# Attention values with V stationary in a two-layer hybrid decoder trunk

## The chip, the cores and the metric

One NeuronCore of a Trainium2 chip runs the whole kernel. The metric is the device time of one execution, in microseconds (us). TensorE (PE) multiplies and writes to PSUM; its weight loads have a row of their own (PEld). VectorE (DVE), ScalarE (ACT) and GpSimd (POOL) do the elementwise work, and SyncE (SP) issues the loads.

## The reference

A trunk of two layers works on x with 256 tokens and 1024 features, in float32. Cut to what matters:

```python
for l in range(DEPTH):                       # 2
    h = _rms_norm(x, attn_norm[l])
    proj = h @ w_in[l]                       # 1720 columns, split into q, six k/v, gates, latents
    o_a = _nsa(q_a, k_cmp, v_cmp, k_s, v_s, k_w, v_w, gates)   # 8 heads, 2 groups, dim 64
    o_b = _mla(c_q, c_kv, k_r, ...)                            # 8 heads, dim 64 + 32
    mixed = concatenate([_rms_norm(o_a, nsa_out_norm[l]), _rms_norm(o_b, mla_out_norm[l])])
    x = x + mixed @ w_out[l]
    h = _rms_norm(x, mlp_norm[l])
    x = x + square(relu(h @ w_ff1[l])) @ w_ff2[l]              # 4096 wide
return _rms_norm(x, final_norm)
```

NSA mixes three branches by gates: compressed blocks (15 positions), selected blocks and a window; with 256 tokens the last two both cover the causal keys. Every softmax divides by its sum, and gates and group norms act on the attention's output.

## The kernel before

Tokens lie in two tiles of 128 (`t` = 0, 1). Every large product is done in three passes: an operand is split into a high part of reduced precision (float32r) and the rest, a low part, and `mm3` (L350) adds high x high, high x low and low x high. Weights stream through one SP queue in tiles of 128 x 1024 (two chunks of 512 columns), `ask` (L314) cuts each into two pieces; ACT writes the high part (L334), DVE or POOL in turn the low part (L336).

A layer projects h by four blocks of columns (`kcs`, `q`, `kw`, `lat`). It puts q and keys through a rotation and transposes them, compresses keys and values with 16 chunks of small matmuls (`hid`, L949; four tiles of 32 columns of the array beside each other), multiplies the latents up (`ups`), and then does the attention. The output projection and the MLP in four quarters (`up`, `down`) follow.

Attention comes in units of four heads or head branches. `units` (L654) computes scores into PSUM banks of 512 columns; `softmax` (L637) takes maxima on DVE (L640) and exponentials on ACT (L646), which stay unnormalised. The unit then transposes each 128 x 128 block of p on TensorE (`trans`, L379), ACT copies it to SBUF, and `nsa_values` (L698) and `mla_values` (L751) multiply with p^T stationary and V moving:

```python
mm(o[:, a, br, :], pts[a // per][:, ((a % per) * 2 + br) * nk + kt, :], V[:, kt, br, g, :], start=kt == 0, stop=kt == nk - 1)
```

V has 64 features and a column of ones, so a product has 65 columns, tokens in the partitions, and the softmax sum in the 65th column. `nsa_after` (L713) and `mla_after` (L764) take the reciprocal (L719, L768), multiply by the gate and scale the output (`otmp`, `ob`), and POOL adds the branches (`oa`). The compressed branch is one product with 512 columns (L622, `cmp_chain`). `group_chain` (L784) sums squares on ACT, takes the root on POOL, multiplies by it and by a row of gains (`mx`, L800), and transposes the result back for the output projection (`split_into`, L389).

`norm` (L417) multiplies x by gains (L425), which are broadcast over the partitions by a DMA (`gain`, L263), and transposes the result.

The order of TensorE and SP is written by the kernel itself. `Driver` (L168) advances chains by rank with a clock of its own: the main chain has rank 9, norms 0, transposes 1, NSA 3 and 4, compressed branch 3.5, MLA 5 and 6. A chain says how long its result will need on the other engines, and that time is multiplied by 1.8. DVE, ACT and POOL are ordered by the framework's scheduler (L1178).

PSUM has two banks for accumulators, three for scores, two for transposes and one (`pv`) for values.

Of the kernel before, what the change touches and what calls it, by code (L numbers as in the profile page):

```python
# [9 lines left out]
F32 = mybir.dt.float32  # L10
# [6 lines left out]
P = 128  # L17
L = 2
# [25 lines left out]

BLOCKS = {
    "kcs": (512, 512),
    "q": (0, 512),
    "kw": (1024, 280),
    "lat": (1304, 416),
# [56 lines left out]
def _plan():  # L106
    plan = []

    def add(chunks, per, n, split=True):
        plan.extend((min(per, chunks - a), n, split) for a in range(0, chunks, per))  # L110

    for name, (_, n) in BLOCKS.items():
        add(KC, PER_TILE[name], n)
    add(1, 1, 1024)
    add(2, 1, 768)
    add(16, 2, 512, False)
    add(16, 2, 512)
    for q in range(NQ):
        add(32, 2, 512)
    return plan  # L120


PLAN = _plan() * L


def _layer_stream(inp, l):
    out = []
    w_in = inp["w_in"][l]
    for name, (a, n) in BLOCKS.items():
        out += _tiles(w_in[:, a : a + n], PER_TILE[name])  # L130
    for name, parts in (("w_kv_up", (64, 64)), ("w_q_up", (NOPE, ROPE))):

        w = inp[name][l].reshape(-1, H, sum(parts))
        w = np.concatenate([w[:, :, : parts[0]].reshape(-1, H * parts[0]), w[:, :, parts[0] :].reshape(-1, H * parts[1])], 1)
        out += _tiles(w, 1)
    out += _tiles(np.concatenate([inp["cmp_w1_k"][l], inp["cmp_w1_v"][l]], 1), 2)
    for i in range(2):
        for nb in range(2):
            out += _tiles(inp["w_out"][l][i * 512 : i * 512 + 512, nb * 512 : nb * 512 + 512], 2)
# [9 lines left out]
def _pack(inp):  # L149
    arr = {"x": inp["x"].reshape(S, D)}  # L150
    arr["wst"] = np.concatenate([t for l in range(L) for t in _layer_stream(inp, l)])
    names = ("attn_norm", "nsa_out_norm", "mla_out_norm", "mlp_norm", "mla_q_norm", "mla_kv_norm")
    arr["gains"] = np.concatenate([np.concatenate([inp[n][l] for n in names]) for l in range(L)] + [inp["final_norm"]])
# [11 lines left out]
GL = 3 * 1024 + 384  # L165


class Driver:  # L168

    def __init__(self, banks):
        self.t = 0.0
        self.chains = []
        self.done = {}
        self.free = {k: [0.0] * n for k, n in banks.items()}
        self.count = 0

    def spawn(self, rank, gen):
        self.count += 1  # L180
        self.chains.append([rank, self.count, self.t, gen, None])

    def event(self, name, after=0.0):
        self.done[name] = self.t + after * 1.8

    def put(self, bank, after):
        self.free[bank].append(self.t + after * 1.8)

    def ready(self, c):
# [8 lines left out]
    def run(self):  # L198
        while self.chains:
            able = [(self.ready(c), c) for c in self.chains]  # L200
            able = [(r, c) for r, c in able if r is not None]
            first = min(r for r, _ in able)
            self.t = max(self.t, first)
# [4 lines left out]
            c[4] = None  # L208
            try:
                kind, *what = next(c[3])  # L210
            except StopIteration:
                self.chains.remove(c)
                continue
            if kind == "pe":
                self.t += what[0]
                c[2] = self.t + what[1] * 1.8
            elif kind == "rank":
                c[0] = what[0]
            elif kind == "until":
                c[2] = what[0]  # L220
            else:
                c[2] = self.t
                c[4] = (kind, what[0])


@with_exitstack
def trunk(ctx: ExitStack, tc: tile.TileContext, x, wst, gains, pos, cw2, cst, out):
    nc = tc.nc
    mm = nc.tensor.matmul
    E = {"v": nc.vector, "g": nc.gpsimd, "s": nc.scalar}.get  # L230

    def copy(eng, dst, src):
        (nc.scalar.copy if eng == "s" else E(eng).tensor_copy)(dst, src)  # L233

    pool = lambda name, n, **k: ctx.enter_context(tc.tile_pool(name=name, bufs=n, **k))
    const = pool("const", 1)
    raw_p = pool("raw", 6)
    wp = pool("wsplit", 6)
    hl = pool("hl", 13)
    gp = pool("gain", 2)  # L240
    tm = pool("tm", 6)
    at = pool("at", 1)
    pp = pool("pp", 4)
    sm = pool("sm", 4)
    BANKS = {"acc": 2, "s": 3, "tr": 2, "pv": 1}
    psum = {k: pool(f"ps_{k}", n, space=bass.MemoryType.PSUM) for k, n in BANKS.items()}
    dr = Driver(BANKS)

    def urgent():
        return tc.high_priority(offset=100)  # L250
# [4 lines left out]
    X = [const.tile([P, D], F32, name=f"x{t}") for t in range(NT)]  # L255
# [943 lines left out]
```

## Time and profile before

| what | value |
|---|---|
| median of 3 runs | 641.09 us |
| the three runs | 646.26, 639.11, 641.09 us |
| profiled execution, its own time | 646.11 us |
| span of its instructions | 644.3 us |
| mean granted clock of TensorE | 0.986 |
| TensorE busy | 621.4 us (96%) |

The span reaches from the first to the last instruction. "Busy" counts time in which at least one instruction of an engine is under way. Matmuls overlap in the pipeline, so their durations add up to more than that, and the price of one in a row of equals is the distance from start to start. The granted clock is a share of 2.4 GHz; the other level is 1.2 GHz.

### The profile page before, as it was taken

What the parts mean: (1) busy time and instruction counts of PE and PEld (TensorE: products, weight loads), DVE (VectorE), ACT (ScalarE), POOL (GpSimd) and SP (SyncE); (2) the same over time, 40 slices, a digit from 0 to 9 for tenths busy, and PEclk for the clock granted to TensorE, in tenths of its full rate; (3) what the DMA queues carried; (4) which work ended last, traced back from release to release, by engine and by line L of the source; (5) the groups of instructions that cost most, each with busy time, mean ns of one, the idle gap of its engine ahead of it and who ended that gap; (6) DMA issues with size and microseconds to landing.
All of it is one profiled execution on the core that took longest, in us unless ns stands there. A gap on an engine that the chain in (4) does not pass through costs nothing.

```text
span 644.3 us, 10909 instructions
## 1 busy us (share of the span) xinstructions
PE 621.4 (96%) x4099; PEld 548.3 (85%) x4099; DVE 420.4 (65%) x665; ACT 354.6 (55%) x735; POOL 300.4 (47%) x298
## 2 busy tenths in 40 slices
PE   7899899999999999999999889999999999999995
PEld 4697688889889899899888768798998998998985
DVE  4797778675656647558677866866664673764662
ACT  5566667565535546355564475765663654554551
POOL 2675404344553645445466631244544554554351
PEclk8899999999999999999999898999999999999998
DMA  8756733155555655745644665114547565565601
GB/s 306 264 175 206 236 116 100 34 198 173 185 169 191 208 182 166 226 155 186 213 126 134 211 212 199 34 66 149 177 142 220 164 200 174 193 204 176 198 1 66
DMA packets 31732, 108.48 MB, mean 168 GB/s; under 512 B 3776, under 2 KB 4416, under 8 KB 31680
## 3 DMA queue, kind: packets, MB, share of 16 engines
q1 hardware_dynamic: 31392, 107.27, 50.8%
q8 instruction: 32, 0.52, 0.3%
q10 hardware_dynamic: 288, 0.52, 0.2%
q14 instruction: 20, 0.16, 0.1%
HBM read 106.73 MB, written 1.05 MB: 167 GB/s over the span
## 4 chain that ended last, share of the span: by engine, by line
PE 85%; DVE 7%; ACT 4%; DMA 3%; issue 1%; SPq 0%; POOL 0%; POOLq 0%; ACTq 0%
PE acc L352 24%; PE acc L354 24%; PE acc L353 24%; PE tr L384 4%; DVE wlo L336 2%; PE pv L708 2%; DMA raw<-in_wst_dram 2%; PE pv L759 2%; ACT whi L334 1%; PE acc L949 1%; PE s L693 1%; DMA x<-in_x_dram 1%; PE s L746 1%; ACT p L646 1%; DVE qmT L233 1%
## 5 line engine op out<-in xcount | busy, mean ns | idle before, releaser
L336 POOL TENSOR_TENSOR wlo<-raw,whi 128x512 fp32r<-128x512 f32 (+3 forms) x178 | 245.0, 1397 | 221.2 <-ACT whi L334 220.9
L334 ACT CAST whi<-raw 128x512 fp32r<-128x512 f32 (+2 forms) x360 | 201.4, 610 | 113.6 <-PE acc L354 74.7
L336 DVE TENSOR_TENSOR wlo<-raw,whi 128x512 fp32r<-128x512 f32 (+3 forms) x182 | 170.5, 973 | 58.4 <-ACT whi L334 58.3
L352 PE MATMUL acc<-h,whi 128*128 128x256 f32 x512 | 145.3, 284 | 0.0
L354 PE MATMUL acc<-h,wlo 128*128 128x256 f32 x512 | 145.0, 283 | 0.0
L353 PE MATMUL acc<-h,whi 128*128 128x256 f32 x512 | 145.0, 283 | 0.0
L352 PE MATMUL acc<-whi,u 128*128 128x512 f32 (+1 forms) x264 | 101.5, 384 | 0.0
L353 PE MATMUL acc<-wlo,u 128*128 128x512 f32 (+1 forms) x264 | 101.2, 383 | 0.0
L354 PE MATMUL acc<-whi,u 128*128 128x512 f32 (+1 forms) x264 | 101.1, 383 | 0.0
L352 PEld LDWEIGHTS acc<-h,whi 128*128 128x128 f32 x512 | 98.3, 192 | 0.2
L353 PEld LDWEIGHTS acc<-h,whi 128*128 128x128 f32 x512 | 98.3, 192 | 0.2
L354 PEld LDWEIGHTS acc<-h,wlo 128*128 128x128 f32 x512 | 98.3, 192 | 0.0
L1057 DVE TENSOR_TENSOR sq<-relu 128x512 f32<-128x512 f32 x32 | 37.2, 1161 | 38.9 <-ACT relu L1053 38.9
L354 PEld LDWEIGHTS acc<-whi,u 128*128 128x128 f32 x264 | 49.6, 188 | 9.8
L353 PEld LDWEIGHTS acc<-wlo,u 128*128 128x128 f32 x264 | 49.7, 188 | 9.4
L352 PEld LDWEIGHTS acc<-whi,u 128*128 128x128 f32 x264 | 49.7, 188 | 9.3
L1029 DVE SCALAR_TENSOR_TENSOR x<-acc,r,x 128x512 f32<-128x512 f32 (+1 forms) x33 | 24.1, 731 | 49.0 <-PE acc L354 49.0
L1053 ACT ACTIVATE relu<-acc 128x512 f32<-128x512 f32 x32 | 19.0, 594 | 59.3 <-PE acc L354 59.3
L352 PE MATMUL acc<-whi,h 128*128 128x512 f32 (+2 forms) x112 | 41.2, 368 | 0.0
L353 PE MATMUL acc<-wlo,h 128*128 128x512 f32 (+2 forms) x112 | 40.2, 359 | 0.2 <-POOL wlo L336 0.2
L354 PE MATMUL acc<-whi,h 128*128 128x512 f32 (+2 forms) x112 | 39.9, 357 | 0.0
L646 ACT ACTIVATE p<-s,nm 128x128 f32<-128x128 f32 (+1 forms) x96 | 33.9, 430 | 7.9 <-DVE nm L640 4.0
(185 smaller groups left out, 913.3 us busy)
## 6 DMA issues: line engine op xcount, KB each, us to landing
raw<-in_wst_dram SPq DMA_DIRECT2D x178, 512.0 KB, 4.2
raw<-in_wst_dram SPq DMA_DIRECT2D x8, 416.0 KB, 3.3
raw<-in_wst_dram SPq DMA_DIRECT2D x4, 420.0 KB, 3.3
raw<-in_wst_dram SPq DMA_DIRECT2D x4, 384.0 KB, 3.1
x<-in_x_dram SPq DMA_DIRECT2D x4, 256.0 KB, 6.3
g_mix<-in_gains_dram SPq DMA_DIRECT2D x2, 512.0 KB, 5.8
g_mlp<-in_gains_dram SPq DMA_DIRECT2D x2, 512.0 KB, 5.1
g_attn<-in_gains_dram SPq DMA_DIRECT2D x2, 512.0 KB, 3.9
```

The lines of the kernel that those rows point to most:

```text
L334: nc.scalar.copy(hi[:, v], r[:, v])
L336: E(eng).tensor_sub(lo[:, v], r[:, v], hi[:, v].bitcast(F32))
L352: mm(acc, ah, wh, start=start, stop=False, **k)
L353: mm(acc, ah, wl, start=False, stop=False, **k)
L354: mm(acc, al, wh, start=False, stop=stop, **k)
L384: nc.tensor.transpose(tr[:rows, c, :], col, ident)
L646: nc.scalar.activation(p[:, k], s[:, k], AF.Exp, bias=nm[:, a : a + 1], scale=scale)
L708: mm(o[:, a, br, :], pts[a // per][:, ((a % per) * 2 + br) * nk + kt, :], V[:, kt, br, g, :], start=kt == 0, stop=kt == nk - 1)
L759: mm(o[:, r, :], pts[r // per][:, (r % per) * nk + kt, :], VM[:, kt, hb * 4 + r, :], start=kt == 0, stop=kt == nk - 1)
L1029: nc.vector.scalar_tensor_tensor(X[t][:, c], acc, scale, X[t][:, c], op0=OP.mult, op1=OP.add)
L1053: nc.scalar.activation(r, acc, AF.Relu)
L1057: nc.vector.tensor_mul(sq, r, r)
```

## The change

**Values.** V becomes the stationary operand and p^T the moving one. Output is feature-major: features in the partitions, tokens in the columns. V fills 64 columns of the array, so the heads of even and odd place go to the two halves (`tile_position`). Selected and window branch, both key tiles and the compressed branch add into one PSUM tile, as gates and 1/sum are multiplied into p before its transpose; the sum comes from the exponential's own accumulator. A unit now has eight head branches (NSA: one group) or four heads (MLA), two units for each `t` and kind.

**Group scale later.** The output is feature-major already and needs no transposes. Gains act per partition at the eviction; the squares are added over features by a matmul against ones, and 1/rms, a number per token, multiplies the output projection's accumulator (`into_x`).

**Gains.** All gains lie in one small table with features in the partitions. The attention gain is multiplied in after the transposes of x, the MLP gain into the rows of the up weights as they are split (ACT scales the high part; a DVE operation makes the low part). Broadcast loads go, but for the last norm.

**Order.** `Driver` now models each operation of DVE, ACT and POOL by a formula (`_cost`), places it in a gap of that engine's time line, and issues all engines' instructions in the order of this plan; some operations choose DVE or POOL by which ends earlier. The order of the projections stays; the up weights are read behind `hid`; the main chain has rank 9 throughout, the compressed branch rank 2. Buffers: 5 raw tiles where there were 6, 8 for temporaries where there were 6, 14 for layer tensors where there were 13.

The diff, cut to its core:

```diff
+RANK = ((3, 4), (5, 6))
...
+MARGIN = 250.0
...
+    if lane == "v":
+        if op == "reciprocal":
+            return 100 + 6.6 * n
+        if op == "scalar_tensor_tensor":
+            return 140 + 1.25 * n
+        if op == "tensor_scalar":
+            return 110 + 0.9 * n
+        return 80 + 1.25 * n
+    if lane == "s":
+        return 125 + 0.77 * n + (190 if kw.get("accum_out") is not None else 0)
...
-    def event(self, name, after=0.0):
-        self.done[name] = self.t + after * 1.8
...
+    def event(self, name):
+
+        self.done[name] = max(self.t, self.last) + MARGIN
...
-                nc.scalar.activation(p[:, k], s[:, k], AF.Exp, bias=nm[:, a : a + 1], scale=scale)
-            dr.put("s", 2300)
+                scalar.activation(p[:, k], s[:, k], AF.Exp, bias=nm[:, a : a + 1], scale=scale, accum_out=den[:, a : a + 1])
+            dr.put("s")
+            vector.reciprocal(den, den)
+            if gate is not None:
+                dg = den.rearrange("p (r b) -> p r b", b=2)
+                vector.tensor_mul(dg, dg, gate)
+            pa = p.rearrange("p (a k) -> p a k", k=width)
+            either.tensor_mul(pa, pa, den[:, :, None].to_broadcast([P, n, width]))
             return p
...
+                for br in range(2):
+                    for kt in range(nk):
+                        for par in range(2):
+                            rows = slice(par * DK, (par + 1) * DK)
...
+                            mm(o[rows], values_of(kt, br, g), p, start=br + kt == 0, stop=False, tile_position=(0, par * DK), skip_group_check=True)
                 for a in range(2):
...
+                    c = g * 2 + a
+                    mm(o[:, a, :], bd["v"][:, 2 * c : 2 * c + 2, :].rearrange("p h d -> p (h d)"), pctT[t], start=False, stop=True, skip_group_check=True)
...
+            scalar.activation(sq, pv, AF.Square)
+            vector.tensor_mul(o, pv.rearrange("p (c n) -> p c n", c=2), gain(l, "mix", 4 * i + 2 * g, 2))
+            scalar.copy(hi, o)
+            either.tensor_sub(lo, o, hi.bitcast(F32))
+            dr.put("pv")
...
+            mm(ss[:, :1], sqs, ones, start=True, stop=True)
...
+                            mm(o[rows, a, :], VM[:, kt, hb * 4 + h, :], pts[0][:, h * nk + kt, :], start=a + kt == 0, stop=kt == nk - 1, tile_position=(0, par * DK), skip_group_check=True)
...
+                    if g is not None:
+                        scalar.activation(hi[:, v], r[:, v], AF.Copy, scale=g)
...
+                    vector.scalar_tensor_tensor(lo[:, v], r[:, v], g, hi[:, v].bitcast(F32), op0=OP.mult, op1=OP.subtract)
...
-    with tc.manual_schedule(engines={mybir.EngineType.PE, mybir.EngineType.SP}):
+    with tc.manual_schedule():
         dr.run()
```

## Rows read from the trace of the kernel before

**Rows 1.** The page, first part: busy us (share of span) x instructions.
```profile
PE 621.4 (96%) x4099; PEld 548.3 (85%) x4099; DVE 420.4 (65%) x665; ACT 354.6 (55%) x735; POOL 300.4 (47%) x298
```
**Rows 2.** Stages in us from the span's start; the first row names the columns.
```profile
core 0: us, PE busy (x) PEld busy (x) DVE busy (x) ACT busy (x) POOL busy (x), PEclk, DMA share, GB/s
0.00:28.00 28.00, 21.72 (x78) 13.91 (x79) 15.26 (x24) 14.61 (x29) 13.34 (x22) 0.88 0.82 298
52.00:150.00 98.00, 93.77 (x728) 80.31 (x727) 71.58 (x157) 62.59 (x153) 38.32 (x46) 1.00 0.45 149
150.00:345.00 195.00, 195.00 (x1211) 175.95 (x1210) 120.81 (x146) 102.56 (x188) 98.11 (x77) 1.00 0.57 182
362.00:400.00 38.00, 34.39 (x314) 27.74 (x315) 25.25 (x60) 22.57 (x61) 10.68 (x15) 0.91 0.64 215
```
**Rows 3.** Waits of TensorE, whole span: us in total, times, longest us.
```profile
PE pv L708 <- DVE otmp L722: 3.6, 2, 1.8
PE s L354 <- DVE h L394: 2.7, 1, 2.7
PE tr L384 <- DVE h L425: 2.6, 2, 1.7
PE tr L384 <- DVE kT L496: 2.3, 1, 2.3
PE pv L622 <- ACT pt L233: 1.7, 2, 0.9
PE tr L384 <- DVE qT L530: 1.3, 1, 1.3
```
**Rows 4.** Groups by line and form, TensorE: count, busy us, mean ns.
```profile
L708 PE MATMUL pv<-V,pt 128*128 128x65 f32 x192 | 24.0, 275 | 3.6 <-DVE otmp L722 3.6
...
L759 PE MATMUL pv<-VM,pt 128*128 128x65 f32 x96 | 11.6, 271 | 0.0
...
L384 PE MATMUL tr<-idt,mx 128*128 128x128 f32 x32 | 4.8, 273 | 0.0
```
**Rows 5.** The chain that ended last: start us, us it holds, what, how many.
```profile
61.32 0.79 PE acc L949 x24
...
78.58 0.44 PE tr L384 x4
79.02 0.36 PE acc L949 x8
...
83.86 1.73 PE pv L708 x16
...
106.61 0.89 PE s L746 x8
...
112.57 0.86 PE s L746 x4
```
**Rows 6.** Groups by line and form, the other engines: busy us, mean ns, idle before.
```profile
L336 DVE TENSOR_TENSOR wlo<-raw,whi 128x512 fp32r<-128x512 f32 x162 | 153.4, 983 | 54.8 <-ACT whi L334 54.7
...
L394 DVE TENSOR_TENSOR h<-tr,h 128x512 fp32r<-128x512 f32 x16 | 11.0, 685 | 5.9 <-ACT h L393 5.9
...
L791 POOL TENSOR_TENSOR oa<-oa,ocg 128x512 f32<-128x512 f32 x4 | 5.1, 1267 | 0.2
...
L376 ACT ACTIVATION_READ_ACCUMULATOR junk<-x 128x1 f32 x21 | 3.9, 188 | 0.0
...
L719 DVE RECIPROCAL wv<-pv 128x4 f32<-128x4 f32 x16 | 2.8, 177 | 8.5 <-PE pv L708 8.4
```
**Rows 7.** Timeline of DVE at the start: start us, us, operation, idle before.
```profile
5.95 0.69 DVE L425 TENSOR_TENSOR h<-x,g_attn 128x512 f32<-128x512 f32 x1 [5.03 <-DMA g_attn<-in_gains_dram]
```

More of the change, by code (lines that the diff above doesn't have):

```diff
@@ L1 @@
+import heapq
+from bisect import bisect
+from collections import deque
 from contextlib import ExitStack
@@ L48 @@
     "kw": (1024, 280),
-    "lat": (1304, 416),
 }
@@ new lines, in start_of, with work @@
+    def start_of(self, key, cost, at):
+        return self.clock[key].find(at, cost)[1]
+    def work(self, key, op, f, out, ins, kw):
+        read = [a for a in (*ins, *kw.values()) if hasattr(a, "tensor")]
+        name = out.tensor.name
+        cost = _cost(key, op, max(_size(a) for a in (out, *read)), kw)
+        at = max([self.t] + [self.ready.get(a.tensor.name, 0.0) for a in (read if name not in self.slots else [*read, out])])
+        at = self.clock[key].place(at, cost)
+        end = at + cost + 90
+        outs = [out] + ([kw["accum_out"]] if kw.get("accum_out") is not None else [])
+        for a in outs:
+            self.ready[a.tensor.name] = max(end, self.ready.get(a.tensor.name, 0.0))
+        for a in (*outs, *read):
+            self.used[a.tensor.name] = max(end, self.used.get(a.tensor.name, 0.0))
+        self.last = max(self.last, end)
+        self.count += 1
+        heapq.heappush(self.held, (at, self.count, lambda: f(out, *ins, **kw)))
@@ new lines, in flush, with pe @@
+    def flush(self, t=float("inf")):
+        while self.held and self.held[0][0] <= t:
+            heapq.heappop(self.held)[2]()
+    def pe(self, cost, out, read):
+        at = max([self.t] + [self.ready.get(a.tensor.name, 0.0) for a in read if a.tensor.name not in self.shared])
+        if at > self.t:
+            self.stalls.append((self.t, at - self.t, "pe", out.tensor.name, read[-1].tensor.name))
+        self.flush(at)
+        self.t = at + cost
+        self.ready[out.tensor.name] = self.t + 180
+        for a in read:
+            self.used[a.tensor.name] = max(self.t + 60, self.used.get(a.tensor.name, 0.0))
@@ new lines, in trunk, with __getattr__, call @@
+    E = {"v": vector, "g": gpsimd, "s": scalar}.get
+    class Either:
+        def __getattr__(self, op):
+            def call(out, *ins, **kw):
+                read = [a for a in (*ins, *kw.values()) if hasattr(a, "tensor")]
+                n = max(_size(a) for a in (out, *read))
+                at = max([dr.t] + [dr.ready.get(a.tensor.name, 0.0) for a in read])
+                end = lambda e: dr.start_of(e, _cost(e, op, n, kw), at) + _cost(e, op, n, kw)
+                return getattr(E("g" if end("g") <= end("v") + BIAS[0] else "v"), op)(out, *ins, **kw)
+            return call
@@ L727, in nsa_lane, with gate @@
[L727 to L737 removed]
+            def gate(b):
+                par, a0 = b
+                h = g * R + a0 * per * 2 + par
+                return gates[t][:, h : h + 2 * per - 1 : 2, 1:3]
```

1202 lines of the change are left out of this document (663 added, 539 removed).

## The prediction

> **What bounds the kernel now.** I read the page's first part, then the table by stage, then what TensorE waits for, and only then single lines. The page [rows 1] shows TensorE busy for 621.4 of 644.3 us, with DVE, ACT and POOL at 65, 55 and 47%. A busy TensorE can hide waits, so the stages come next [rows 2]. From 150 to 345 us, the MLP of layer 0, TensorE is busy for 195.00 of 195.00 us at full clock while no other engine is above 62%: nothing that happens on DVE, ACT or POOL there can shorten the kernel, and only less TensorE work could. Time is lost in three places. In the start (0 to 28 us) TensorE is idle for 6.3 us, and the granted clock of 0.88 costs 0.12 x 28 = 3.4 us more. In the attention stretch of layer 0 (52 to 150) it is idle for 98 - 93.8 = 4.2 us. In that of layer 1 (362 to 400) it is idle for 38 - 34.4 = 3.6 us, and the clock of 0.91, one stretch at the lower level of 1.2 GHz behind waits, costs 0.09 x 38 = 3.4 us. The waits [rows 3] name the causes: values matmuls behind the eviction of the units before them (`otmp`, 3.6 us), key transposes behind DVE (2.3 and 1.3), the compressed values behind an ACT copy (1.7), and two in the start (2.7 and 2.6). With some 1.3 us of the key wait that lie before 362, the middle has about 12 us to give, the start at most 9.7.
>
> So the bound is TensorE's instruction stream, and the question is what the change takes out of it, and whether the other engines' new order opens more waits than it closes.
>
> **Values with V stationary.** Duration of a matmul in the trace includes its pipeline, so I price by distance in the chain [rows 5]. The old product has 65 moving columns, far too few: 16 records take 1.73 us, 0.108 each, as much as a record of 128 moving columns (8 in 0.89 us, 0.111 each). A float32 matmul leaves two records. Removed [rows 4]: 192 records of L708 and 96 of L759 at 0.108, that is 20.8 and 10.4 us; and 32 transposes of the normalised group at 0.44/4 = 0.11, 3.5 us. Together 34.7 us.
>
> Added, NSA: a layer has 2 groups x 2 branches x 2 head parities = 8 matmuls for t = 0 and 16 for t = 1, each of 256 moving columns, so 96 records in both layers. Alone, such a record takes 0.86/4 = 0.215 [rows 5], 20.6 us in all; but V fills only 64 columns of the array, and the two parities take its two halves. Added, MLA: likewise 96 records, of 128 columns, 10.7 us alone at 0.111. Whether halves run side by side is the disputed price. The nearest row is the compression matmul at L949, four tiles of 32 columns of the array: 24 records take 0.79 us and 8 take 0.36, so 8 more cost 0.215, or 0.027 each, a quarter of the 0.111 that one alone would take. Four tiles run at once; I take two to do so as well: 10.3 + 5.3 us, with 20.6 + 10.7 as the other end and no reason for less than half.
>
> The same rows give the price of entering and leaving that mode: 0.36 - 0.215 = 0.145 us a visit. The change makes 16 visits (4 units for each t and layer): 2.3 us; 0 and 2 x 2.3 are the bounds. The Trainium skill, "TensorEngine Tiling (Array Packing)", Tiling Modes, says that a change of tiling mode drains TensorE; the trace agrees, and a sum without that rule would be 2.3 us better.
>
> The sum of squares over features is now a matmul against ones: 8 in all, 16 records at 0.111, 1.8 us. The compressed branch goes from one product with 512 columns to four with 128, the same columns, nothing. Transposes of x stay, only without a multiplication before them. Added in sum 10.3 + 5.3 + 2.3 + 1.8 = 19.7; **TensorE's stream gets 34.7 - 19.7 = 15.0 us shorter**. It is bound by itself, so this shows in the time, unless new waits eat it.
>
> **The start.** The first multiplication by a gain waits 5.03 us for a broadcast row of gains [rows 7]; now x is transposed as it lands, and the gain comes from a small table at the eviction. 0.5 MB of broadcast leaves the first loads too, 1.7 us at the 298 GB/s of that stage [rows 2]. But 1 MB of x and 2 MB of the first projection's weights must still land, 10 us at that rate, and the first pair waits for the second half of the rows. Bounds: a loss of 3 us (if the constants, which the mask copy on DVE awaits, come later) and a gain of 8; I take 4.
>
> **The other engines.** Each of 36 score banks gets more: the exponentials' sums (96 reads at 0.188 us on ACT, 18 us), a reciprocal (0.177), for NSA a gate product, and one 128x512 product p x 1/sum on DVE or POOL [rows 6]. In return the work after the values goes: `otmp`, `ob`, `ocg`, `mx` and the low part, 8 x 256 + 4 x 256 + 2 x 512 + 4 x 512 + 4 x 512 = 16 x 512 columns a layer on DVE, and `oa` on POOL. ACT's squares and high parts stay what they are in columns. By layer ACT gets 48 x 0.188 = 9.0 us. DVE gets, if POOL takes nothing, 18 products at 0.685 (the rate of L394), 30 reciprocals and gates at 0.177, and 8 evictions with two passes of 256 columns and sums of 0.5: 12.3 + 5.3 + 9.5 = 27, less 16 x 0.685 + 20 x 0.177 = 14.5; so 12.5 us. Set against the 62.6 us of ACT and 71.6 of DVE in the 98 us of layer 0 [rows 2], with some 87 us left for the stretch (98 less half of the 15 and some waits), ACT stands at 82%, DVE at 97%, and POOL, at 38 us, is free for what is moved. So no engine becomes the bound if the plan shifts work to POOL, but the slack is thin.
>
> The price of a DVE product is itself in dispute. Reading PSUM, DVE takes 0.685 for 128x512 (L394); with both inputs in SBUF it takes 0.983 on average (L336) [rows 6]. The Trainium skill, "SBUF — State Buffer", Who interferes with whom, says that a DVE instruction with two SBUF inputs and a GpSimd instruction that reads SBUF shut each other out. The rows agree so far as L336 is dearer by 0.3 us; by that rule the 36 products would cost 35.4 us of DVE and not 24.7. On POOL such a product takes 1.267 (L791).
>
> In the MLP the gain moves into the split of the weights: all low parts of up tiles go to DVE and nearly all others to POOL. DVE had 120.8 us of 195, ACT 102.6, POOL 98.1 [rows 2], so work is shifted between engines at 50 to 62%, up to six tiles ahead. Cover is ample, so 0; if the cover were gone, a late low part would cost its 0.98 us.
>
> **The order.** Before, the wait times given to the TensorE order were stretched by 1.8 and the other engines' order came from elsewhere; now one plan gives all, with 250 ns of margin. A good plan removes most of the 12 us in the middle; a tight one adds waits where DVE is late. Bounds: 12 us gained to 12 lost; I take 6 gained, half, since the causes named in [rows 3] (long DVE queues ahead of a transpose) are what such a plan sees, while DVE's dearer products are what it doesn't: it prices them at 80 + 1.25 x 512 = 720 ns.
>
> **The sum.** 15.0 + 4 + 6 = 25 us. The profiled execution took 646.1 us (span 644.3, 1.8 around it), the slowest of those shown; the median is 641.1. From 646.1 it gives 621.1, from the median 616.1. I predict **616 us**.
>
> **Rivals.**
> *The plan closes nearly all waits.* Start 8 and middle 12 gained: 15 + 20 = 35, 606 us. For it: the waits have few causes, and out projection and up projections are there as filler. Against: loads in the start. Chance 0.25.
> *The order gives nothing.* Only TensorE's work falls, and waits grow by up to 5 us: 626 to 631 us. For it: ACT and DVE get fuller. Chance 0.20.
> *The halves don't run side by side.* 10.3 + 5.3 us more: 632 us. Against it: L949. Chance 0.08.
> *The normalised p is late* (slower). The product stands between exponential and transposes. A bank then comes later by reads, reciprocal, gate and product, 2 x 0.188 + 2 x 0.177 + 0.983 = 1.7 us, on a DVE that is full. If TensorE has nothing ready in 15 of the 36 banks, that is 26 us, which eats the 25; with 20 banks it is 34, and 616 + 34 = 650 us. Against it: units of four kinds lie side by side, and main work fills. Chance 0.08.
> My forecast has 0.39, its own range 610 to 622.
>
> A measurement of this kernel tells about 1% from no change (its three runs spread by 1.1%). Faster by over 1% (under 634.7): all of the first four cases but the edges, 0.84; within 1%: 0.08; slower: 0.08. The range for 8 in 10 reaches down past the good plan and up past the halves: 602 to 638.
>
> **What would show it.** Right: values records of 256 columns at about half of 0.215 us' distance, TensorE's busy time near 600 us, no rows for transposes of `mx`, the MLP still without idle time, TensorE's waits in the middle of 6 us or less. Wrong: values at 0.215; transposes of `p` waiting for DVE or POOL by more than 10 us in total; TensorE idle in the MLP behind low parts; a longer stretch at 1.2 GHz in either attention stage; a first projection that starts later than 10 us.

## The result, and the profile after

The changed kernel takes 671.09 us (median of 3 runs, 669.05 to 672.6) where the kernel before takes 641.09: ratio 1.0448, interval 1.0342 to 1.0554. It is 30 us slower; 25 us faster was forecast.

The first rows of the page of the kernel after answer to [rows 1]; the last one shows the chain that ended last, by engine (in the same row before: PE 85%, DVE 7%, ACT 4%):

```profile
span 669.3 us, 10994 instructions
PE 627.4 (94%) x4011; PEld 541.5 (81%) x4011; DVE 443.3 (66%) x674; ACT 364.3 (54%) x818; POOL 344.2 (51%) x329
...
PE 77%; POOL 7%; DVE 6%; ACT 3%; issue 3%; DMA 3%; SPq 0%; POOLq 0%; ACTq 0%; DVEq 0%
```

TensorE is busy for 6 us more, but that is no sign of more work. Take the span apart. Idle time is the span less the busy time: 644.3 - 621.4 = 22.9 us before [rows 1], 669.3 - 627.4 = 41.9 after. Time lost to the clock is the span times what the mean granted clock is short of 1: 0.014 x 644.3 = 9.0 before (clock 0.986), 0.040 x 669.3 = 26.8 after (0.960). What is left is work at the full 2.4 GHz: 612.4 before, 600.6 after. So TensorE did get 11.8 us less to do, and lost 19.0 us by idling and 17.8 by the clock. Where the clock is low while TensorE idles, this way counts the time twice. Taken over its busy time alone, the clock costs 6.6 us before and 22.9 after in the two traces, and the work falls by 10.3 us. So read 10 to 12 us of work saved.

Where, the table by stage of the kernel after shows (it answers to [rows 2]; a row begins with the stretch in us). The stretches are, for each layer, from the last compression product to the first output product ("the middle"), from there to the first product of the MLP ("the end"), and the MLP of layer 0:

```profile
core 0: us, PE busy (x) PEld busy (x) DVE busy (x) ACT busy (x) POOL busy (x), PEclk, DMA share, GB/s
78.00:116.00 38.00, 27.23 (x153) 22.57 (x154) 30.64 (x68) 22.63 (x64) 19.86 (x18) 0.80 0.35 115
116.00:158.00 42.00, 42.00 (x249) 31.91 (x250) 28.16 (x53) 21.91 (x59) 17.17 (x21) 0.94 0.28 89
158.00:345.00 187.00, 186.90 (x1191) 169.63 (x1190) 121.19 (x138) 100.27 (x174) 87.32 (x66) 1.00 0.56 183
400.00:442.00 42.00, 32.63 (x165) 27.26 (x164) 30.00 (x71) 23.97 (x70) 22.90 (x21) 0.72 0.34 113
442.00:482.00 40.00, 39.37 (x248) 30.65 (x248) 28.13 (x53) 21.66 (x58) 17.37 (x21) 1.00 0.35 106
```

The same two middles and ends in the kernel before, in the same view:

```profile
80.60:115.00 34.40, 33.23 (x258) 29.62 (x251) 26.89 (x75) 22.70 (x57) 10.76 (x12) 1.00 0.28 101
115.00:143.50 28.50, 28.50 (x159) 24.28 (x157) 18.86 (x32) 16.42 (x37) 11.45 (x15) 1.00 0.39 129
394.30:428.60 34.30, 33.13 (x257) 29.52 (x250) 26.80 (x75) 22.59 (x56) 10.75 (x12) 1.00 0.29 98
428.60:457.50 28.90, 28.83 (x160) 24.39 (x158) 19.97 (x32) 16.59 (x37) 11.39 (x15) 1.00 0.39 126
```

The MLP is as full as before. Before, the middle had 1.2 us of idle time in each layer and the full clock. After, it has 10.8 and 9.4 us of idle time, and its clock costs 0.20 x 38 = 7.6 and 0.28 x 42 = 11.8 us (some of it in the idle time). The middle holds 153 matmul records in place of 258 in layer 0; what left it was in part removed and in part comes later, in the end, which grew from 28.5 to 42 us. Attention of both layers is where the time went: the first product of the MLP starts 14 us later than before in layer 0 (157.7 against 143.5 us) and 24 us later in layer 1 (481.9 against 457.5).

The waits of TensorE in the middle of layer 0 (in total, times, longest), after:

```profile
PE tr L643 <- ACT pt L305: 4.2, 1, 4.2
PE tr L643 <- POOL p L305: 1.9, 1, 1.9
PE acc L440 <- DVE rb L305: 1.3, 1, 1.3
PE pv L440 <- DVE kcmp L305: 1.2, 1, 1.2
```

No one cause dominates: a transpose of p stands behind a late copy to SBUF, another behind the normalising product, the latents' queries and the compressed values behind DVE. The chain of the same stretch (start, us it holds, what) shows what they have in common:

```profile
83.18 1.35 DVE wlo L305
84.53 0.96 DVE sg L305
85.51 0.96 DVE sg L305
...
87.24 2.14 DVE wlo L305 x2
89.38 0.10 DVE kcmp L305
89.48 1.34 DVE wlo L305
90.82 0.33 DVE ra L305
91.15 0.34 DVE rb L305
```

From 83.2 to 91.5 the path that sets the end runs on DVE: the rows shown are 7.5 us of it, and 4.8 of these are low parts of weights that stand in DVE's queue between the small steps of the compression and of the rotation. Added up over the whole stretch, the rows of this view put the chain on DVE for 17.1 of 38 us; in the same view of the kernel before, from 80 to 115 us, they put it there for 5.6 of 35, and on TensorE for 17.5 (11.5 of 38 after). So before the change, too, TensorE held only half of the path through this stretch, although it was busy nearly all the time.

### The profile page after: what moved, and what is told of

Its sections match the earlier page's. It is cut to its first block, busy times and chain, and to the rows that moved or that the text cites. A ratio compares the mean times of both kernels' runs of the same rounds, so it can differ in the third digit from the quotient of the medians.

```text
span 669.3 us, 10994 instructions
## 1 busy us (share of the span) xinstructions
PE 627.4 (94%) x4011; PEld 541.5 (81%) x4011; DVE 443.3 (66%) x674; ACT 364.3 (54%) x818; POOL 344.2 (51%) x329
## 4 chain that ended last, share of the span: by engine, by line
PE 77%; POOL 7%; DVE 6%; ACT 3%; issue 3%; DMA 3%; SPq 0%; POOLq 0%; ACTq 0%; DVEq 0%
PE acc L440 66%; PE pv L440 5%; PE tr L643 3%; POOL wlo L305 3%; PE s L440 3%; DMA raw<-in_wst_dram 2%; POOL FT L305 2%; DVE wlo L305 2%; ACT whi L305 1%; DMA x<-in_x_dram 1%; ACT p L305 1%; POOL ra L305 1%; DVE sq L305 1%; POOL h L305 0%; DVE sg L305 0%
## 5 line engine op out<-in xcount | busy, mean ns | idle before, releaser
L440 PE MATMUL acc<-h,whi 128*128 128x256 f32 x1024 | 185.0, 283 | 0.0
L440 PEld LDWEIGHTS acc<-h,whi 128*128 128x128 f32 x1024 | 160.1, 192 | 0.7
L440 PE MATMUL acc<-whi,u 128*128 128x512 f32 (+1 forms) x528 | 160.6, 383 | 0.0
L305 DVE TENSOR_TENSOR wlo<-raw,whi 128x512 fp32r<-128x512 f32 (+4 forms) x87 | 112.4, 1306 | 18.8 <-ACT whi L305 17.4
L305 ACT CAST whi<-raw 128x512 fp32r<-128x512 f32 (+4 forms) x211 | 112.8, 601 | 5.0 <-DMA raw<-in_wst_dram 3.4
L305 ACT ACTIVATE whi<-raw,gcols 128x512 fp32r<-128x512 f32 x128 | 85.2, 715 | 51.4 <-PE acc L440 47.4
L305 DVE SCALAR_TENSOR_TENSOR wlo<-raw,gcols,whi 128x512 fp32r<-128x512 f32 x128 | 103.2, 860 | 10.0 <-ACT whi L305 10.0
L305 POOL TENSOR_TENSOR p<-p,dn 128x512 f32<-128x512 f32 x35 | 38.6, 1106 | 47.5 <-DVE dn L305 42.7
L440 PE MATMUL acc<-whi,m 128*128 128x512 f32 x128 | 47.4, 419 | 0.0
L440 PEld LDWEIGHTS acc<-whi,h 128*128 128x128 f32 x224 | 41.5, 193 | 3.9
```

The source lines that it names most:

```text
L305: heapq.heappush(self.held, (at, self.count, lambda: f(out, *ins, **kw)))
L440: nc.tensor.matmul(out, lhsT, rhs, **k)
```

## The experiments

Each run is timed against the kernel before on the same chip; the ratio to it is given, with its interval, and the kernel after stands at 1.0448 (1.0342 to 1.0554). A difference in us is a difference of ratios times 641, unless said otherwise.

One caution holds for most of the runs. TensorE's order is written by the driver or by the plan, from costs, ranks and due times, so an edit of any of these writes a new order as well. In the traces only e2, e11 (but for its filling), e19 and e20 keep TensorE's order of the kernel after, and only e4 that of the kernel before.

**First guesses: one edit, one culprit.** The change also moved the up weights behind the compression weights in the stream, gave the order of all engines to the plan, and let POOL take the products. One run each:

```diff
@@ e1 @@
+STREAM = ("kcs", "q", "kw", "lat", "ups", "hid")
...
-    for name in ORDER:
+    for name in STREAM:
...
+                up_weights.extend([list(weights(1)), list(weights(2))])
                 yield from hidden()
@@ e2 @@
-    with tc.manual_schedule():
+    with tc.manual_schedule(engines={mybir.EngineType.PE, mybir.EngineType.SP}):
@@ e3 @@
-BIAS = (1000.0, 1500.0, 0.0)
+BIAS = (-1000.0, 1500.0, 0.0)
@@ e4, in the kernel before: plan of the stream, then its use @@
+    add(16, 2, 512, False)
     add(1, 1, 1024)
     add(2, 1, 768)
-    add(16, 2, 512, False)
...
-        wkv = list(weights(1))
-        wq = list(weights(2))
...
+        wkv = list(weights(1))
+        wq = list(weights(2))
         for t in range(NT):
             yield need("latT", t)
```

> The changed kernel with one edit: the three tiles of the latent up projections stand ahead of the compression weights in the stream and are split ahead of the compression matmuls, as in the kernel before. Theory 1 (between the end of the compression matmuls and the output projection TensorE starves for these weights, 20 us idle in both layers, and falls to 1.2 GHz behind that, 20 us more): idle time in that stage drops to 8 us or less in both layers together, the clock's loss to 6 or less, 671 -> about 645 us (637 to 652). Theory 2 (the plan's order of DVE, ACT and POOL is at fault everywhere): at most 6 us better, 665 or more. Theory 3 (products sent to POOL are at fault): no better than 665.

> The changed kernel with one edit: only TensorE and SyncE keep the order of the plan; DVE, ACT and POOL are ordered by the framework's scheduler, as before. Theory 2: most of the loss goes, 650 us or less. Theory 1: the weights still come late, 660 or more. Theory 3: the choice of POOL stays, 665 or more.

> The changed kernel with one number changed: an operation that may go to DVE or POOL goes to POOL only where the plan has it end 1 us earlier there (before: unless it ends 1 us later). Theory 3: the waits of TensorE for kd, qr and p on POOL (10.6 us in all) go and the clock's loss with them, 655 us or less. Theory 1 and 2: within 5 us of 671, as DVE gets what POOL loses.

> The kernel before with the reverse of the first edit alone: the up projections' tiles stand behind the compression weights in the stream. Theory 1: the same stage, 1.2 us idle a layer before, starves by 4 to 8 us a layer, and 641 -> 650 to 660 us. Theory 2 and 3: within 3 us of 641, as the order of the engines and the use of POOL stay.

Measured: e1 672.78 us, 1.0437 (1.0372 to 1.0503); e2 700.09, 1.0870 (1.0800 to 1.0940); e3 681.16, 1.0563 (1.0499 to 1.0627); e4 638.9, 0.9936 (0.9894 to 0.9977). None of the three theories got its gain. The place of the up weights does nothing after the change, and in the kernel before the later place is even a little better: 638.9 us, 0.6% under the kernel before (0.2 to 1.1%), the fastest of this study. With TensorE's order of the plan kept, the plan's order of the other engines is 27 us better than the framework's. Products on DVE, with the new order that this brings, are no better than on POOL (e3; the intervals touch).

**Waiting for the compressed branch.** After the change the compressed branch adds into the same accumulator as the other two, so the NSA values wait for it; the first stand at 105 us (the timeline's first row of `pv<-pt,kv`). e5 takes the wait away, e6 moves the compression up, e7 keeps the computation whole but adds the compressed branch later, and e9 is e6 and e7 together:

```diff
@@ e5 @@
-            if i == 0:
-                yield need("pct", t)
...
-                    mm(o[:, a, :], bd["v"][...], pctT[t], start=False, ...)
+                    mm(o[:, a, :], idt, idt, start=False, ...)
@@ e6 @@
-ORDER = ("kcs", "q", "kw", "lat", "hid", "ups")
+ORDER = ("kcs", "q", "hid", "kw", "lat", "ups")
@@ e7, behind the values of the other branches @@
+                scalar.copy(part, pv)
+                dr.put("pv")
+                yield need("pct", t)
+                yield "get", "pv"
...
+                    mm(pv[:, a * P : a * P + P], bd["v"][...], pctT[t], start=True, stop=True, ...)
+                vector.tensor_add(part, pv, part)
...
```

> The NSA values multiply constants in place of the compressed values and probabilities, same instructions, and no longer wait for them (the output lacks the compressed branch). Theory W (after the change the compressed branch adds into the same PSUM accumulator as the other two branches, so the first NSA values stand at 105 us where they stood at 65, and TensorE lacks work from 76 to 100 and from 400 to 430): first values near 70 us, TensorE's idle 18 to 26 us in place of 35, clock loss 10 to 18 in place of 27, time 640 to 656 us. Rival R (the longer chain from scores to transposes, with its accumulate reads, reciprocals, gates and POOL products, sets the pace): first values earlier, but time within 6 us of 671.

> Only the order of the weight blocks: the compression weights directly behind q, ahead of kw and lat. Theory W: the hidden layer ends some 10 us earlier against the NSA scores, and kw and lat cover its chain; time 650 to 664 us. Rival R: within 6 us of 671.

> The whole computation, but the compressed product has an accumulator of its own and is added on VectorE when it comes; values of the other two branches wait for nothing but their probabilities. Costs 8 copies of 256 columns on ScalarE and 8 additions on VectorE more. Theory W: first values near 70 us, time 642 to 658 us, a few us over the run without the wait. Rival R: 668 to 678 us.

> The compression weights directly behind q and the compressed product added later. Theory W: the wait is gone already with the second, so the order adds little: 640 to 658 us. Rival R: 665 to 678 us.

Measured: e5 668.58 us, 1.0358 (1.0301 to 1.0416); e6 674.78, 1.0462 (1.0404 to 1.0519); e7 665.37, 1.0304 (1.0237 to 1.0372); e9 673.06, 1.0432 (1.0373 to 1.0491). In e7 the values start at 69 us, and the time falls by 0.0144 x 641 = 9 us of 30. In e5 it falls by 6. Both intervals still touch that of the kernel after, and both runs have a new order. The middles of e7:

```profile
77.20:116.60 39.40, 30.87 (x194) 25.72 (x186) 31.43 (x72) 25.07 (x76) 20.64 (x19) 0.83 0.35 120
400.90:440.80 39.90, 31.53 (x197) 26.09 (x185) 30.75 (x74) 25.54 (x75) 21.39 (x20) 0.84 0.33 113
```

The values moved, but the stage takes 39.4 and 39.9 us where it took 38 and 42, with 8.5 and 8.4 us of idle time. So the wait was real, and it isn't what sets the length of the middle.

**Margin, clock, softmax, cover.** Four runs about what that is:

```diff
@@ e10 @@
-MARGIN = 250.0
+MARGIN = 1000.0
@@ e11, where the plan sees TensorE pause in attention @@
+            if self.fill:
+                self.fill(int((at - self.t - 150.0) / 60.0))
...
+            nc.tensor.matmul(pvs[:, 3 * P :], zero, zero, start=True, stop=True, ...)
@@ e12 @@
-            vector.reciprocal(den, den)
...
-            either.tensor_mul(pa, pa, den[:, :, None].to_broadcast([P, n, width]))
@@ e14, in the kernel before, for NSA and MLA values @@
-                        for kt in range(nk):
+                        kt = 0
...
-                return 4 * nk * 107
+                return 4 * 107
```

> One number: the plan lets a result be used 1000 ns, not 250 ns, after its own forecast of its end. Theory M (the plan is too tight: vector work ends later than it thinks, so TensorE stands before instructions that were put too early while later ones could run): TensorE's idle under 28 us in place of 35, time 650 to 664 us. Rival L (TensorE lacks work in the middle of attention whatever the order, because the chains there are longer than the work that is left beside them): 668 to 684 us.

> In attention, from the compression layer on, every pause that the plan forecasts for TensorE is filled with matmuls of zeros by zeros (some 200 a layer, 128 columns each, about 12 us a layer at 2.4 GHz), into columns that nobody reads. Theory C (the idle time costs twice: the clock falls to its lower level in and behind it, and the work that follows takes twice as long; clock loss is 27 us after the change and 9 before): the clock stays at its higher level in the middle, clock loss under 15 us, time 648 to 662 us although TensorE does more. Rival L (the chains between the engines set the end, TensorE's speed there doesn't): 668 to 676 us with the clock up. If the filling comes where there is no pause: 678 to 690 us.

> Left out: the reciprocals of the sums, the gate products and the product of the probabilities with them (36 products of 512 columns, nearly all on POOL at 1.05 us, that stand between exp and the transposes); the output lacks the division and the gates. Theory N (the longer chain from scores to transposes is what holds TensorE): time 648 to 660 us, idle under 27 us. Rival L2 (other chains, from hidden layer to compressed values and from latents to keys and queries, hold it): 664 to 671 us.

> The kernel before, with the value products of the second key tile left out (a third of them: 96 of 288 records, 6.9 us at the mean of 72 ns of the rows); softmax, transposes and everything else stay, and the output lacks those keys. Theory L (the value products were the cover of chains that are as long as the work beside them, so that taking them away gives little): 1 to 3 us less than before. Rival P (before is bound by TensorE's work, and the loss after the change comes from the new order alone): 5 to 8 us less than before.

Measured: e10 679.18 us, 1.0553 (1.0489 to 1.0617); e11 675.01, 1.0491 (1.0436 to 1.0545); e12 659.03, 1.0241 (1.0183 to 1.0299); e14 642.39, 0.9983 (0.9941 to 1.0025).

A wider margin doesn't help. The filling of e11 raised the mean clock from 0.960 to 0.982; its middles, and the end of layer 1:

```profile
78.00:121.00 43.00, 37.36 (x363) 33.28 (x355) 30.89 (x68) 22.51 (x64) 20.08 (x18) 0.88 0.30 102
405.00:446.00 41.00, 34.94 (x361) 30.26 (x358) 30.56 (x71) 23.81 (x70) 23.04 (x21) 1.00 0.33 114
446.00:486.00 40.00, 39.32 (x250) 30.67 (x251) 26.77 (x53) 21.49 (x58) 17.48 (x21) 1.00 0.31 106
```

In layer 1 TensorE runs the middle at full clock, with more than twice the records, and the stage takes 41 us where it took 42; in layer 0 the clock is 0.88 where it was 0.80, and the stage takes 43 us where it took 38. So theory C's 648 to 662 us didn't come: with a higher clock the time is no better. That the clock by itself costs nothing isn't shown, since the filling takes time too, some 25 us at full clock, of which idle time took 8 (41.9 before the filling, 33.8 with it). In one stretch the clock did cost: the records that the kernel after takes from 415.7 to 431.4 us, mostly at half the clock, took 12.5 us in e11 and not 15.7.

e14 asks the same of the kernel before. It takes away 96 records, which at the prediction's 0.108 are 10.4 us (the 72 ns a record of its expectation is too low: in the trace they start 0.110 apart). This gave back 0.0017 x 641 = 1 us (4 at most by the interval). Before, TensorE had hardly any idle time in the middle, and yet it wasn't alone on the path, as its 17.5 us of the chain's 35 say as well. That the chains over the other engines were as long as its work is argued from these two and not shown: each unit of e14 reports a shorter time to the driver, so that TensorE's order changed too, and a worse order can hide a gain. e12 says what made the chains longer: without the normalising, 0.0207 of the time, 13 us, comes back. TensorE's idle time fell only from 41.9 to 37.1 us in it; theory N had expected a fall of 8 or more.

**The same from the other side.** Theory S is now that the longer softmax lengthened chains that were already as long as TensorE's work. e15 takes the sums away too. e16 gives the kernel before the new softmax, without the gates, and leaves TensorE's work as it was. e18 and e8 test a second part: the change lets the latent projection come behind the NSA scores (rank 9, before 2.5).

```diff
@@ e15, beside the edit of e12 @@
-... AF.Exp, bias=nm[:, a : a + 1], scale=scale, accum_out=den[:, a : a + 1])
+... AF.Exp, bias=nm[:, a : a + 1], scale=scale)
@@ e16, in the kernel before @@
+            ... AF.Exp, ..., accum_out=den[:, a : a + 1])
+            nc.vector.reciprocal(den, den)
...
+            nc.gpsimd.tensor_mul(pa, pa, den[:, :, None].to_broadcast([P, n, width]))
...
-                    when.append(dr.t + 1610 * 1.8)
+                    when.append(dr.t + 2710 * 1.8)
@@ e18, in the kernel before @@
-        yield "rank", 2.5
@@ e8, beside the edit of e7 @@
+                if name == "lat":
+                    yield "rank", 2.5
...
```

> As e12_no_normalise, and the exps don't sum: the 96 reads of accumulators (some 220 ns each on ScalarE, 21 us in both layers) go too; the output lacks the sums, the division and the gates. Theory S (the softmax chain as a whole is what the change lost on): 644 to 653 us. Rival T (what remains above before comes from the later latents, the feature-major steps behind the values and the plan's order): 655 to 661 us.

> The kernel before, with the softmax of the kernel after: exps that sum, reciprocals, and a product of 512 columns on POOL for every score bank ahead of its transposes; transposes are allowed 2 us later, the computation is whole, and TensorE's work is that of before. Theory S (softmax chain, whatever the order): 652 to 668 us. Rival T: 641 to 649 us, since before's order has other work to put there.

> The kernel before, with the latent projection at the rank of the other projections, behind the NSA scores, as the change has it. Theory T (later latents make the middle of attention longer): 646 to 658 us. Rival S: within 3 us of before.

> The kernel after, with the latent projection back at the rank of before, ahead of the NSA scores, and the compressed product added later as in e7_compressed_added_later (665 us). Theory T: 648 to 660 us. Rival S: 662 to 672 us.

Measured: e15 673.22 us, 1.0479 (1.0381 to 1.0577); e16 662.87, 1.0331 (1.0252 to 1.0411); e18 658.67, 1.0276 (1.0198 to 1.0354); e8 665.03, 1.0377 (1.0295 to 1.0458).

In e16 nothing is taken from TensorE, the whole computation stays, and the kernel before loses 0.0331 x 641 = 21 us. But the transposes' later due time moves some 380 of TensorE's 4099 records to another place, from 62 us on, so the 21 us are the softmax and a new order together. First its middles, by stage, then the added product and the added reads (count, busy us and mean ns of one):

```profile
76.40:125.20 48.80, 41.80 (x294) 35.79 (x287) 38.04 (x97) 29.83 (x97) 25.44 (x29) 0.93 0.23 84
399.00:446.40 47.40, 41.82 (x296) 36.03 (x288) 35.00 (x93) 29.23 (x94) 23.00 (x27) 0.92 0.19 67
```

```profile
L651 POOL TENSOR_TENSOR p<-p,dn 128x512 f32<-128x512 f32 x36 | 37.3, 1044 | 31.5 <-DVE dn L649 27.1 <-DVE otmp L726 2.0 <-DVE wc L624 1.7
L647 ACT ACTIVATION_READ_ACCUMULATOR p<-s,nm 128x1 f32 x96 | 20.3, 211 | 0.0
```

The middle grows from 34 to 48 us, in part because it holds more: 294 records where it held 258 in layer 0. Its idle time is 7.0 and 5.6 us where it was 1.2, and its clock 0.93 and 0.92. POOL, where the product lies, is busy for 25 of 49 us, so that it was not full; that the banks' later transposes did it, and not the load, is argued from this.

e18 shows that the latents' place, with the order that follows from it, costs 18 us in the kernel before: its middles,

```profile
78.80:125.50 46.70, 40.24 (x281) 35.28 (x272) 31.10 (x82) 24.23 (x61) 12.34 (x15) 0.93 0.26 91
398.60:443.00 44.40, 38.66 (x282) 33.71 (x270) 30.40 (x81) 23.72 (x59) 12.34 (x15) 0.96 0.26 95
```

have 6.5 and 5.7 us of idle time. But giving the old rank back in the kernel after (e8) gained nothing on e7. And e15 took 15 us more than e12 with less to do. Both edits let the plan write a new order, so an order can be worth that much by itself, whatever it was made for, and what a run with a new order shows is uncertain by as much.

**In one and the same order.** The last two runs therefore keep the place of every instruction on every engine, by letting the plan count what isn't issued:

```diff
@@ e19 @@
-        heapq.heappush(self.held, (at, self.count, lambda: f(out, *ins, **kw)))
+        if not self.plan_only:
+            heapq.heappush(self.held, (at, self.count, lambda: f(out, *ins, **kw)))
...
+            dr.plan_only = True
             vector.reciprocal(den, den)
...
+            dr.plan_only = False
             return p
@@ e20, beside it @@
+        if op == "activation" and AF.Exp in ins:
+            kw = {k: v for k, v in kw.items() if k != "accum_out"}
```

> The kernel after with every instruction in the place that its plan gave it, but without the 36 products on the probabilities, the 36 reciprocals and the 24 gate products (the output lacks the division and the gates): e12_no_normalise let the plan make a new order, this doesn't. Theory S (the longer softmax is the larger part of the loss): 650 to 660 us. Rival O (12 us of e12 came from the luck of another order): 663 to 671 us.

> As e19_same_order_no_products, in the same order, and the 96 exps don't sum either (no accumulator reads on ScalarE; the output lacks the sums too). Theory S: 2 to 8 us under e19, since the reads lie in the same chain; that e15 took 673 us was its new order. Rival O: within 2 us of e19.

Measured: e19 660.63 us, 1.0232 (1.0167 to 1.0296); e20 658.18, 1.0210 (1.0163 to 1.0258). e19, 0.6 us above theory S's range, agrees with e12, and it is the clearest run of the study: the normalising takes 0.0216 x 641 = 14 us in the order of the kernel after (10.5 by the times alone; 6 to 22 by the two intervals). The middles of e19, which lie between the same TensorE instructions as in the kernel after:

```profile
78.80:113.70 34.90, 27.80 (x166) 22.25 (x158) 25.35 (x60) 20.95 (x62) 11.35 (x11) 0.80 0.39 132
397.40:431.90 34.50, 28.03 (x180) 23.31 (x169) 24.87 (x58) 22.24 (x67) 14.88 (x14) 0.85 0.38 133
```

They took 38 and 42 us after the change. Leaving the products out makes each bank's way to its transposes shorter and takes 38.6 us of work off POOL as well; After the change POOL was busy for 19.9 of the 38 and 22.9 of the 42 us, about half, so the shorter way is the likelier reason, but no run separates the two. What e20 has over e19, 1 to 2 us, lies within the intervals; that the sums cost anything of their own isn't shown.

**Account.** Of the 30 us lost, 10 to 14 are shown to be the normalising between exponentials and transposes. The wait for the compressed branch may be 6 to 9 more (e5, e7, in new orders). The rest stays open: the latents behind the scores can cost that much (e18), but with the plan's order no run gave it back. No run tested the low parts of weights in DVE's queue, on which the chain of the middle lay, by an edit of their own. Of the 10 to 12 us that TensorE saved, none shows up.

## Why the prediction was wrong

**What bounds the kernel now: wrong in the step to the attention.** The text read [rows 2] as 93.77 of 98 us busy and concluded that the bound was TensorE's instruction stream. For the MLP that held. For attention a busy engine only said that it had work to put beside the chains. The chain of the kernel before, on TensorE for 17.5 of 35 us between 80 and 115, says so, and e14 points the same way, in a new order: some 10 us less work, 1 us less time. (A small slip beside it: the profiled execution, at 646.1 us, wasn't the slowest shown; one run took 646.26.)

**Values with V stationary: right in the prices, wrong in their worth.** What was removed had the price that was taken: the old records start 0.110 us apart in the trace. The halves of the array do run side by side. The timeline of TensorE after shows 16 records of 256 columns in one visit:

```profile
443.59 1.08 PE L440 MATMUL pv<-pt,kv 128*64 128x256 f32 x8 [0.64 <-DVE rm L305]
444.50 1.03 PE L440 MATMUL pv<-pt,kw 128*64 128x256 f32 x8
445.47 0.71 PE L440 MATMUL pv<-pct,bdv 128*128 128x128 f32 x4
```

From 443.59 to 445.47 they take 1.88 us, 0.118 a record where half of 0.215 was taken; the 0.16 us above 16 x 0.1075 is the visit, priced at 0.145. The stream got 10 to 12 us shorter by the account above, 15.0 were forecast. The step that failed is the sentence behind it: "It is bound by itself, so this shows in the time, unless new waits eat it." The sum gave new waits no term: the longer way from exponentials to transposes stood in it at nothing. New idle time took 19.0 us and the clock 16 to 18, and the normalising alone, left out in the same order, is worth 10 to 14 (e19).

**The start: right up to 28 us, and lost again behind it.** From 0 to 28 us TensorE lost 6.3 + 3.4 = 9.7 us before [rows 2]. After, the same stretch and the next one read as in the first two rows here; the third is the next one before:

```profile
0.00:28.00 28.00, 22.73 (x88) 15.48 (x89) 10.91 (x16) 14.40 (x28) 18.91 (x25) 0.94 0.70 240
28.00:52.00 24.00, 19.24 (x105) 15.73 (x105) 19.97 (x27) 12.03 (x27) 23.28 (x30) 0.95 0.42 136
28.00:52.00 24.00, 24.00 (x141) 21.55 (x140) 22.34 (x48) 14.23 (x36) 16.35 (x23) 1.00 0.55 183
```

The first is 5.3 us of idle time and 0.06 x 28 = 1.7 of clock, 2.7 us better than before; 4 were forecast. But from 28 to 52 us TensorE now idles for 4.8 us, where it didn't idle at all, and the clock takes 1.2. Its waits there are transposes behind rotated queries and keys, 3.7 us of them behind POOL, which is busy for 23.3 of 24 us: the rotation of the queries stands there behind 10.3 us of additions for the compression (35.2 to 45.5 us). So by 52 us the start was 3 us worse than before. e3, which prefers DVE, idles for 6.3 us in this stretch; no run put the rotation back on DVE alone.

**The other engines: right in the load, wrong in the question.** The text asked whether an engine becomes full, found DVE at 97% at worst and POOL free, and gave the softmax additions no term in the sum. Their prices were near. The rows of the kernel after answer to [rows 6]:

```profile
L305 POOL TENSOR_TENSOR p<-p,dn 128x512 f32<-128x512 f32 x35 | 38.6, 1106 | 47.5 <-DVE dn L305 42.7 <-PE acc L440 1.9 <-ACT pt L305 1.9
L305 ACT ACTIVATION_READ_ACCUMULATOR p<-s,nm 128x1 f32 x96 | 21.1, 219 | 0.0
L305 DVE TENSOR_TENSOR wlo<-raw,whi 128x512 fp32r<-128x512 f32 x65 | 90.1, 1394 | 18.3 <-ACT whi L305 17.4 <-POOL whi L305 0.7
```

The plan gave 35 of 36 products to POOL at 1.106 us (1.267 was the nearest row), and a read costs 0.219 us (0.188). DVE is busy for 30.64 of 38 us in the middle, 81%, so it isn't full. What counts, by e19, is more likely how long a bank takes from its scores to its transposes, and that grew by reads, reciprocal, gate and product. The low parts that DVE still makes in this form went from 983 to 1394 ns each on average; over half of them lie in the two MLPs, where TensorE has hardly any idle time.

**A price in dispute.** With the products on DVE (e3) the groups of that run give

```profile
L305 DVE TENSOR_TENSOR p<-p,dn 128x512 f32<-128x512 f32 x36 | 28.5, 792 | 1.2
```

792 ns on average, between the 685 and 983 that the prediction set against each other. The Trainium skill, "SBUF — State Buffer", Who interferes with whom, has DVE instructions with two SBUF inputs and GpSimd's SBUF reads shut each other out; a share of the dearer price fits that, but no run here had DVE alone.

**The order: wrong in sign.** "Bounds: 12 us gained to 12 lost; I take 6 gained." The middles have 18 us more idle time than before (10.8 + 9.4 against 1.2 + 1.2). The waits that the text priced lay ahead of that, and there the plan did close most of them: before, after, and after in layer 1 (to [rows 2], last row):

```profile
52.00:80.60 28.60, 25.54 (x268) 19.91 (x266) 21.02 (x45) 19.49 (x54) 12.87 (x16) 1.00 0.70 224
52.00:78.00 26.00, 25.77 (x257) 20.91 (x257) 17.13 (x47) 19.66 (x76) 14.42 (x20) 0.98 0.53 168
362.00:400.00 38.00, 34.98 (x318) 29.27 (x316) 27.27 (x61) 24.39 (x85) 27.40 (x39) 1.00 0.46 152
```

Idle time fell from 3.1 to 0.2 us up to the middle of layer 0, and from 362 to 400 us the clock is full where it was 0.91. Behind it the plan opened more than it had closed. Two of its decisions may have weighed 6 to 9 us (values behind the compressed branch, e5 and e7) and up to 18 (latents behind the scores, e18), each with a new order in it. The text priced neither, though the diff shows both.

**The rivals.** The normalised p that comes late, at 0.08, named a mechanism that the runs bear out. Its price, 1.7 us a bank in 15 banks, 26 us, is about twice the 10 to 14 of e19; the 21 of e16 are nearer, but hold a new order. What made the chance too small was "main work fills": in the middle the main work is the latents' and compression's own chains, which wait too. Its 650 us was 21 too low although its own price was too high, since it kept all 25 us of gains. That it was the rival nearest to the result is in part luck: it says nothing of the other half of the loss. The range, 602 to 638, rested on the same belief in these gains.

**What would show it.** Three signs of being right came true: values records at half of 0.215 us, no transposes of `mx`, an MLP without idle time. But TensorE's busy time is 627.4 us and not near 600, its waits in the middle are over 6 us, and there are longer stretches at 1.2 GHz in both attention stages. The first projection starts at 10.5 us, after the 10 named, but it did so before (10.3). Transposes of p waited for POOL by 3.7 us in the whole span, less than the 10 us named: here the lateness was spread over many waits, and none of them alone looks guilty.

## What to carry to other kernels

Before pricing less work on an engine that is 96% busy, ask how long the chains beside it are. If they are about as long as its work, saving work may give little and a longer chain can cost at once, as here. Give every step that is added to a chain a term in the sum, even where no engine becomes full. A test is cheap: take a few us of the engine's work out of the old kernel and see whether the time follows. But keep the order of all instructions in such a test, or it measures the order too: two orders of this plan differed by 15 us (e12, e15).

## What was not expected of the hardware

TensorE can be busy and yet be left at the lower clock. Stretches of the kernel after, by stage:

```profile
400.00:416.00 16.00, 10.10 (x51) 8.12 (x50) 12.96 (x28) 12.88 (x37) 12.39 (x12) 0.75 0.58 197
416.00:430.00 14.00, 13.32 (x55) 12.08 (x56) 8.00 (x22) 3.98 (x10) 5.78 (x5) 0.50 0.37 114
430.00:442.00 12.00, 9.21 (x62) 7.06 (x62) 9.03 (x21) 7.10 (x24) 4.73 (x5) 0.93 0.00 0
```

From 400 to 416 us TensorE is busy for 10.1 of 16 us, and the clock falls; from 416 to 430 it is granted 0.50, that is 1.2 GHz, though it is busy for 13.3 of 14 us. How much a busy time is worth there shows in one visit of values records in layer 0, at the lower clock:

```profile
117.59 1.98 PE L440 MATMUL pv<-pt,kv 128*64 128x256 f32 x8
119.35 1.92 PE L440 MATMUL pv<-pt,kw 128*64 128x256 f32 x8
121.20 0.71 PE L440 MATMUL pv<-pct,bdv 128*128 128x128 f32 x4
```

From 117.59 to 121.20 the 16 records take 3.61 us, where the same visit in layer 1, shown above, took 1.88. So a busy share says little of the loss until the granted clock is read beside it.
